# Queries and keys of the first attention group as seven products of quarters, and products added onto each other in their PSUM banks

## The chip, the core and the metric

The kernel is one launch on one core of a Trainium2 chip. A core has five engines with a queue each: TensorE (PE, matmuls; the loads of its stationary operand are shown as PEld), VectorE (DVE), ScalarE (ACT), GpSimd (POOL) and SyncE (SP), whose queue issues most of the DMAs. Each engine works its queue off in order; semaphores order the engines among each other. Matmuls write into PSUM banks of 128 x 512 float32, which DVE and ACT read; everything else lies in SBUF tiles of 128 partitions. The metric is the device time of the launch in microseconds (us), the median of several runs. A profiled execution of the same program gives the trace.

## What is computed

A decoder layer on 512 tokens of width 1024: a normed input u goes through one wide projection, whose columns are queries, keys and values of 18 attention heads in three groups of six (dilations 1, 4 and 16), a pooling branch, a state-space branch and gates; the branches are gated, added and projected, and a gated feed-forward block with a short convolution follows. What matters here is the projection of the queries, keys and values and what follows it:

```python
u = rmsnorm(x, ln1_g[i])
proj = u @ w_in[i]
q, k, v, pool_in, z, xbc, dt_raw, gate_pre = jnp.split(proj, split_idx, axis=-1)
...
scores = jnp.einsum("bhnqd,bhnkd->bhnqk", qb, kb).astype(jnp.float32) * scale + bias[:, None]
```

The result is wanted in float32 precision. Each matmul operand is therefore split into a high part (rounded to the matmul's input format) and a low part (the rest), and a product is three matmuls: high by high, high by low, low by high (`mm3`, line 229).

## The kernel before

**Jobs.** The program is a list of jobs (`program`, line 1423), most of them a block of weights with the matmuls that use it. While job n runs on PE, `prepare` (line 1641) makes the low part of job n+1's weights (`low`, L216, DVE), casts the high part of job n+2 in two halves (`cast`, L196, ACT; the halves are put after the next two steps of the job), and starts the DMA of job n+3 (`fetch`). A job may have a `form`, which is called ahead of its cast and names the tile that its weights come from, and a `then`, called behind its low part. The weight tiles rotate: two raw, three high, two low.

**Steps.** Each job calls `step` (line 157) once or more. A step advances the side work, generators in `waiting` and `running`: attention items, pooling, the state-space scan, sums. The engines' queues hold this work in the order in which the Python program records it, for PE, ACT, DVE and POOL alike. SP's queue alone is ordered by the framework.

**Seven products for eight.** A product of two matrices that are cut into quarters takes eight products of quarters, or seven of sums and differences of quarters. Here the token sides are quarters of u (256 tokens by four blocks of 128 rows) and their sums. `sums_of_u(p)` (line 403) makes them for the block pair p = 0 to 3: two reads `uf` (high plus low, L408), four half-width sums `sa` and `sb` (L326 to L329, DVE), two casts to the high parts `sah`, `sbh` (L332, L333, ACT) and two low parts `sal`, `sbl` (L335, L336, DVE). On the weight side the sums are differences of two raw quarters (`diff`, L341, DVE) of 128 x 1536 elements; the two right quarters are loaded into two tiles `w3` of a pool of two (`ypool`), the left ones are fetched as jobs' raw weights.

Two places run seven products before the change:

- `v_pair` (line 608) with `sevens` (line 344): the values of groups 1 and 2, one as left half and one as right half. A job is 2 x 12 matmuls of 384 columns, with weights moving. Its outputs are scattered by DMA (L627, SP) into the tiles `vr` in the order of the dilated groups.
- `qk_sevens(1)` (line 650): queries (left) and keys (right) of group 1. A job is 3 x 12 matmuls of 256 columns.

Each product goes to a PSUM bank of its own; ACT copies some into SBUF tiles `r1`, `r2`, `r5`, and DVE adds the others to them and adds the sums into the output tiles. Groups 0 and 2 use `qk_jobs` (line 631) instead: six chunks of 24 matmuls of 512 columns each; ACT writes the queries, scaled by 0.125, and DVE the keys.

**The order around the change.** The program runs the pooling projection (four jobs of two chunks m; the first two are unrolled in the kernel's opening), the values of group 0 (`v_jobs(0)`, two jobs of 400 columns, four banks), the queries and keys of group 0, the pooling's output, `w_b`'s branch with group 0's attention beside it, four chunks of gates, the pair of values, group 1's queries and keys, and so on. The sums of u are recorded beside `w_b`'s branch, from its fourth job on. The pooling of a chunk (`pool_evac`, line 852) is a copy `pu` on ACT, then a chain of sums and short copies `psw` on POOL (two to nine operations, longer for later chunks), and two steps later `pd` (L869, DVE), a cast `pdh` (L871, ACT) and `pdl` (L872, DVE).

PSUM has two rings of four banks: `MM` for the large products and `SM` for the small ones. SBUF tiles of the side work come from a ring of 54.

Of the kernel before, what the change touches and what calls it, by code (L numbers as in the profile page):

```python
# [83 lines left out]
def trunk(ctx: ExitStack, tc, out, x, rel_bias, ln1_g, w_in, b_gate, w_a, pool_w, pool_scale, w_b,  # L84
# [255 lines left out]
    def diff(out, a, b):  # L340
        dve.tensor_tensor(out, a, b, OP.subtract)  # L341
        return out

    def sevens(quarter, c, side, W, emit):

        r1, r2, r3, r5 = {}, {}, {}, {}

        def job(j, load, form, use):  # L350
            def body(ws):
                wh, wl = ws
                parts = side(j)
                for i in range(2):
                    ps = MM("pb")
                    o = slice(i * P, (i + 1) * P)
                    mm3(ps[:, :c], lambda k: wh[:, k, :], lambda k: wl[:, k, :],
                        lambda k: parts[k][0][:, o], lambda k: parts[k][1][:, o], range(4), flip=True)
                    use(i, ps[:, :c])
                step()  # L360
            new = Job([load] if load is not None else [], 4, c, body)
            new.form = form
            if load is None:
                new.load = lambda: None
            return new

        def keep(r, name):
            def use(i, ps):
                r[i] = T(name)[:, :c]
                act.copy(r[i], ps)  # L370
            return use

        def p5(i, ps):
            keep(r5, "r5")(i, ps)
            dve.tensor_tensor(r2[i], r2[i], ps, OP.add)

        def p6(i, ps):
            dve.tensor_tensor(r1[i], r1[i], ps, OP.add)
            emit(0, 1, i, r1[i], r2[i])

        def p7(i, ps):
            r3[i] = T("r3")[:, :c]
            dve.tensor_tensor(r3[i], r1[i], ps, OP.add)
            emit(1, 1, i, r3[i], r5[i])

        one = job("A11", quarter(0, 0), None, keep(r1, "r1"))
        two = job("A12", quarter(1, 0), None, lambda i, ps: emit(0, 0, i, r1[i], ps))
        three = job(4, None, lambda: W[1], keep(r2, "r2"))
        one.then = lambda: diff(one.raw, W[0], one.raw)
        three.then = lambda: diff(W[0], W[1], W[0])  # L390
        two.then = lambda: diff(W[1], W[1], one.raw)
        yield one
        yield three
        yield two
        yield job(1, None, lambda: one.raw, p5)
        yield job(2, None, lambda: W[1], p6)
        yield job(3, None, lambda: W[0], p7)
        yield job("A22", None, lambda: diff(two.raw, two.raw, W[1]),
                  lambda i, ps: emit(1, 0, i, r3[i], ps))

# [18 lines left out]
    QUARTER = {"A11": (0, LO), "A12": (1, LO), "A22": (1, HI)}  # L419

# [187 lines left out]
    def v_pair():  # L608

        c, W = C_V + 384, []  # L610
        rows_ = lambda c0: w_in[:, c0:c0 + 384].rearrange("(k two p) c -> two p k c", two=2, p=P)
        quarter = lambda two, h: rows_(c + 384 * h)[two]

        def load():
            for two in range(2):
                W.append(ypool.tile([P, 4, S], F32, name="w3", tag="xs")[:, :, :384])
                sp.dma_start(W[two], quarter(two, 1))

        def emit(hi, right, i, a, ps):
            g, tb = 1 + right, 2 * hi + i  # L620
            t = T(f"v{g}")
            dve.tensor_tensor(t[:, :384], a, ps, OP.add)

            for n in range(4):
                if (g, n) not in V:
                    V[g, n] = T(f"vr{g}")
                sp.dma_start(V[g, n][32 * tb:32 * tb + 32, :384], t[n:P:4, :384])  # L627

        return load, sevens(quarter, 384, side_u, W, emit)
# [20 lines left out]
    def qk_sevens(g):  # L650


        W = []
# [3 lines left out]
        r1, r2, r3, r5 = {}, {}, {}, {}  # L657

        def load():
            for two in range(2):  # L660
                W.append(ypool.tile([P, 4, S], F32, name="w3", tag="xs")[:, :, :384])
                sp.dma_start(W[two], quarter(two, 1))

        def job(j, raw, form, use):
            def body(ws):
                wh, wl = ws
                parts = side_u(j)
                for i, ms in enumerate(chunks):
                    ps = MM("pq")
                    for n, m in enumerate(ms):  # L670
                        o = slice(m * P, (m + 1) * P)
                        mm3(ps[:, 256 * n:256 * n + 256], lambda k: wh[:, k, o], lambda k: wl[:, k, o],
                            lambda k: parts[k][0], lambda k: parts[k][1], range(4))
                    use(i, ps[:, :256 * len(ms)])
                step()
            new = Job([raw] if raw is not None else [], 4, 384, body)
            new.form = form
            if raw is None:
                new.load = lambda: None
            return new  # L680

        def keep(r):
            def use(i, ps):
                r[i] = T("rq")[:, :ps.shape[-1]]
                act.copy(r[i], ps)
            return use

        def emit(which, hi, i, a, b):

            for n, m in enumerate(chunks[i]):  # L690
                if (which, g, m) not in QK:
                    QK[which, g, m] = T(f"{which}{g}")
                view = (grouped if which == "q" else plain)(QK[which, g, m], g)
                piece = lambda t: perm(t[:, 256 * n:256 * n + 256], g)
                dve.tensor_tensor(view[:, :, 64 * hi:64 * hi + 64], piece(a), piece(b), OP.add)

        def p5(i, ps):
            keep(r5)(i, ps)
            dve.tensor_tensor(r2[i], r2[i], ps, OP.add)

        def p6(i, ps):
            dve.tensor_tensor(r1[i], r1[i], ps, OP.add)
            emit("k", 0, i, r1[i], r2[i])

        def p7(i, ps):
            r3[i] = T("rq")[:, :ps.shape[-1]]
            dve.tensor_tensor(r3[i], r1[i], ps, OP.add)
            emit("k", 1, i, r3[i], r5[i])

        one = job("A11", quarter(0, 0), None, keep(r1))  # L710
        two = job("A12", quarter(1, 0), None, lambda i, ps: emit("q", 0, i, r1[i], ps))
        three = job(4, None, lambda: W[1], keep(r2))
        one.then = lambda: diff(one.raw, W[0], one.raw)
        three.then = lambda: diff(W[0], W[1], W[0])
        two.then = lambda: diff(W[1], W[1], one.raw)
        return load, [one, three, two, job(1, None, lambda: one.raw, p5), job(2, None, lambda: W[1], p6),
                      job(3, None, lambda: W[0], p7), job("A22", None, lambda: diff(two.raw, two.raw, W[1]),
                                                          lambda i, ps: emit("q", 1, i, r3[i], ps))]

    def attend(g):  # L720
# [7 lines left out]
        def item(h, nb, bank):  # L728
# [21 lines left out]
            if g == 0 and total == 384:  # L750
                dve.tensor_tensor(sb[:, :256], ps[:, :256], b, OP.add)
                dve.tensor_tensor(sb[:, 256:384], ps[:, 256:384], b[:, P:], OP.add)
# [3 lines left out]
            else:  # L756
                n = len(bank)
                dve.scalar_tensor_tensor(sb.rearrange("p (n c) -> p n c", n=n),
                                         ps.rearrange("p (n c) -> p n c", n=n), 0.125 if g == 1 else 1.0,
# [663 lines left out]
    def program():  # L1423
        yield from jobs_a(w_in, C_POOL, 8, uhk, ulk, KD, pool_evac)
        yield Call(lambda: waiting.append(rows_of_bias()))
        yield from v_jobs(0)
        yield from qk_jobs(0)
        yield from pool_out_job()
        yield Call(lambda: attend(0))
        yield Call(lambda: waiting.insert(3, ssd_prep()))  # L1430
        for i, job in enumerate(branch_jobs(1, w_b, YB, 8, more=range(7))):
# [269 lines left out]
```

## Time and profile before

| | us |
|---|---|
| Median of 3 runs (1032.75 to 1033.57) | 1032.86 |
| The profiled execution | 1032.69 |
| Its span, first to last instruction | 1030.9 |
| Mean granted PE clock | 0.999 |

The page names engines as above; L12 is line 12 of the kernel. A row of a timeline gives the start, the duration, the engine, the line, the operation, `out<-in` by the program's names, sizes, and in brackets how long the engine had waited before it and for whom. Operations of one engine overlap by some 0.1 us at their ends, so that the pitch from start to start is shorter than the duration. A row of grouped instructions gives the count, the busy time and the mean of one in nanoseconds. A row of windows gives each engine's busy time in the stretch.

### The profile page before, as it was taken

To read this page: it belongs to the slowest core of one execution; us is meant where nothing else is said; L and a number is where in the kernel's file an instruction comes from. 1 tells how busy PE (TensorE), PEld (TensorE's weight loads), DVE (VectorE), ACT (ScalarE), POOL (GpSimd) and SP (SyncE) were. 2 spreads that over 40 slices of the span, in tenths; PEclk is the share of its full clock that TensorE was granted. 3 is DMA by queue.
4 is the path that set the end of the run, shared out by engine and by line. 5 is a ranking of instruction groups with operands and counts; after the bars stand their busy time and mean duration, and the time that the engine had idled before them with its cause. 6 is when DMAs were issued, how large, how long until landed. Compare 5 with 4: busy or idle time off the path is not lost.

```text
span 1030.9 us, 13254 instructions
## 1 busy us (share of the span) xinstructions
PE 1019.8 (99%) x5276; PEld 858.0 (83%) x5276; DVE 702.7 (68%) x932; ACT 490.2 (48%) x784; POOL 132.8 (13%) x114
## 2 busy tenths in 40 slices
PE   8999999999999999999999999999999999999997
PEld 8998877899888887788888888898888888888885
DVE  6553566788756648666688856767778668685756
ACT  6432545454674363567575324545444434433434
POOL 1770000000000001100044501101111100111002
PEclk9999999999999999999999999999999999999999
DMA  8444312034322354551253625543232233421322
GB/s 270 135 129 137 108 57 75 31 88 138 123 82 82 93 158 108 133 144 44 80 151 128 203 82 203 171 142 121 82 122 83 84 117 112 138 82 41 123 82 82
DMA packets 113357, 117.62 MB, mean 114 GB/s; under 512 B 5236, under 2 KB 97207, under 8 KB 113296
## 3 DMA queue, kind: packets, MB, share of 16 engines
q1 hardware_dynamic: 112703, 115.92, 36.4%
q8 instruction: 41, 0.67, 0.3%
q10 hardware_dynamic: 592, 0.86, 0.2%
q14 instruction: 21, 0.16, 0.1%
HBM read 112.97 MB, written 2.22 MB: 112 GB/s over the span
## 4 chain that ended last, share of the span: by engine, by line
PE 91%; DVE 4%; ACT 3%; issue 1%; DMA 1%; ACTq 0%; DVEq 0%
PE pa L237 30%; PE pu L237 22%; PE pb L237 12%; PE pd L237 7%; PE pqk L237 6%; PE pa L1552 2%; PE pq L237 2%; PE pu L1356 1%; PE ps L743 1%; PE pt L772 1%; PE ppw L237 1%; PE po L784 1%; DVE xs L1133 1%; DVE wl L216 1%; PE py L1057 1%
## 5 line engine op out<-in xcount | busy, mean ns | idle before, releaser
L216 DVE TENSOR_TENSOR wl<-raw,wh 128x2048 fp32r<-128x2048 f32 (+3 forms) x95 | 220.3, 2320 | 53.3 <-ACT wh L196 43.5
L196 ACT CAST wh<-raw 128x1024 fp32r<-128x1024 f32 (+3 forms) x188 | 187.6, 1017 | 48.3 <-DVE raw L341 18.0
L1251 DVE SCALAR_TENSOR_TENSOR hc<-pu,fcol,hc 128x510 f32<-128x510 f32 x88 | 65.8, 748 | 56.0 <-ACT hc L1248 54.4
L237 PE MATMUL pa<-uh,wh 128*128 128x512 f32 x384 | 98.4, 398 | 0.0
L237 PE MATMUL pa<-ul,wh 128*128 128x512 f32 x384 | 94.9, 389 | 0.0
L237 PE MATMUL pa<-uh,wl 128*128 128x512 f32 x384 | 94.8, 389 | 0.0
L237 PEld LDWEIGHTS pa<-ul,wh 128*128 128x128 f32 x384 | 72.1, 188 | 15.1
L237 PEld LDWEIGHTS pa<-uh,wl 128*128 128x128 f32 x384 | 72.1, 188 | 15.0
L237 PE MATMUL pu<-uh,wh 128*128 128x512 f32 (+1 forms) x352 | 83.6, 379 | 0.0
L237 PE MATMUL pu<-uh,wl 128*128 128x512 f32 (+1 forms) x352 | 83.5, 379 | 0.0
L237 PE MATMUL pu<-ul,wh 128*128 128x512 f32 (+1 forms) x352 | 83.5, 379 | 0.0
L237 PEld LDWEIGHTS pa<-uh,wh 128*128 128x128 f32 x384 | 70.3, 188 | 14.8 <-issue 1.0
L237 PEld LDWEIGHTS pu<-ul,wh 128*128 128x128 f32 x352 | 64.2, 188 | 12.5
L237 PEld LDWEIGHTS pu<-uh,wl 128*128 128x128 f32 x352 | 64.2, 188 | 12.5
L237 PEld LDWEIGHTS pu<-uh,wh 128*128 128x128 f32 x352 | 64.1, 188 | 12.4
L1248 ACT ACTIVATE hc<-pu,fcol,fcol 128x512 f32<-128x512 f32 x40 | 31.2, 780 | 80.5 <-PE pu L237 80.5
L1256 POOL TENSOR_TENSOR hc<-hc 128x512 f32<-128x512 f32 x22 | 30.8, 1402 | 289.1 <-DVE hc L1251 252.0
L1025 POOL TENSOR_TENSOR xd<-xc,dtz 128x512 f32<-128x512 f32 x6 | 6.4, 1063 | 355.9 <-issue 307.5
L765 ACT ACTIVATE sb<-sb,nmls 128x128 f32<-128x128 f32 (+1 forms) x72 | 30.1, 419 | 30.4 <-DVE nmls L762 17.7
L1149 ACT ACTIVATE sg<-pa,col 128x512 f32<-128x512 f32 x24 | 16.5, 688 | 45.5 <-PE pa L237 45.4
L1253 ACT ACTIVATE hc<-hc 128x512 f32<-128x512 f32 x22 | 13.9, 632 | 39.9 <-DVE hc L1251 39.9
L907 DVE SCALAR_TENSOR_TENSOR xs<-pa,col,xs 128x509 f32<-128x509 f32 (+2 forms) x24 | 18.0, 749 | 18.7 <-ACT xs L903 18.2
(373 smaller groups left out, 1868.0 us busy)
## 6 DMA issues: line engine op xcount, KB each, us to landing
raw<-in_w_in_dram SPq DMA_DIRECT2D x25, 1024.0 KB, 5.5
raw<-in_ffn_w_up_dram SPq DMA_DIRECT2D x22, 1024.0 KB, 5.2
raw<-in_w_o_dram SPq DMA_DIRECT2D x8, 1024.0 KB, 6.6
raw<-in_ffn_w_down_dram SPq DMA_DIRECT2D x8, 1024.0 KB
raw<-in_w_in_dram SPq DMA_DIRECT2D x14, 512.0 KB, 3.9
raw<-in_w_in_dram SPq DMA_DIRECT2D x6, 768.0 KB
raw<-in_w_b_dram SPq DMA_DIRECT2D x4, 1024.0 KB, 5.2
al<-ad SPq DMA_DIRECT2D x16, 256.0 KB, 7.7
```

The lines of the kernel that those rows point to most:

```text
L196: act.copy(job.high[:, :, o], job.raw[:, :, o])
L216: (eng or dve).tensor_tensor(l[:, :, o], job.raw[:, :, o], h[:, :, o].bitcast(F32), OP.subtract)
L237: pe.matmul(ps, l, r, start=first and n == 0, stop=last and n == total - 1, skip_group_check=onto)
L743: pe.matmul(pss[i][:, o:o + w * P], q[r, n * P:(n + 1) * P], k[r, kb * P:(kb + w) * P], start=True, stop=True)
L765: act.activation(sb[:, off:off + w * P], sb[:, off:off + w * P], AF.Exp, bias=nm[:, n, h:h + 1], accum_out=ls[:, n, h:h + 1])
L907: dve.scalar_tensor_tensor(t[:, sh:], ps[:, :S - sh], col[:, o_cw + 12 * k + m:o_cw + 12 * k + m + 1], t[:, sh:], OP.mult, OP.add)
L1149: act.activation(s, ps, AF.Sigmoid, bias=col[:, o:o + 1])
L1248: act.activation(t, ps, AF.Identity, bias=ff["c1"][:, ff["b"] + m:ff["b"] + m + 1], scale=fw(2, m))
L1251: dve.scalar_tensor_tensor(t[:, sh:], ps[:, :S - sh], fw(k, m), t[:, sh:], OP.mult, OP.add)
L1253: act.activation(t, t, AF.Silu)
L1256: pool.tensor_tensor(a, a, t, OP.mult)
L1552: pe.matmul(first[2 * n + j][:, lo:hi], a[:, k, j * P:(j + 1) * P], b[:, k, lo:hi], start=a is wh and b is uh and k == 0, stop=a is wl and ...
```

## The change

`sevens` and the old body of `qk_sevens` go; both users now call one function, `in_banks`. It keeps four banks for its seven jobs: two A (the two halves of the product's output) and two B. The seven products come in another order, and those that have a part in common are added onto each other in the bank: B takes product 5, then product 3 onto it, later product 2 afresh; A takes product 1, then 6, 7 and 4 onto it. Behind each half product the bank is read: `outs` copies it into the output tile (ACT) where it is the first part of that output, and adds it there (DVE) where it is the second. The differences of weights (`diff`) are called between the first and the second half of a job, and the first of them by a call of its own, ahead of the job before.

Group 0's queries and keys now take this way too, in place of `qk_jobs(0)`. For that the sums of u are made a first time already during the pooling projection (from its fourth job on); they are made a second time at the old place. Group 0's weight quarters are loaded by two calls behind the pooling, and each later user loads its quarters by two calls. The scaling by 0.125 moves for group 0 into the operation that adds the bias to the scores.

```diff
+    def in_banks(quarter, c, outs, chunks=None):
+        W, A, B = [], [], []
+        def load():
+            two = len(W)
+            W.append(ypool.tile([P, 4, S], F32, name="w3", tag="xs")[:, :, :c])
+            sp.dma_start(W[two], quarter(two, 1))
+        def job(j, raw, form, banks, use, onto=False, between=None):
+            def body(ws):
+                wh, wl = ws
+                parts = side_u(j)
+                if not A:
+                    for b in (B, A):
+                        b.extend(MM("pq") for _ in range(2))
+                for i in range(2):
+                    for n, m in enumerate(chunks[i] if chunks else (i,)):
+                        o = slice(m * P, (m + 1) * P)
+                        if chunks:
+                            mm3(banks[i][:, 256 * n:256 * n + 256], lambda k: wh[:, k, o],
+                                lambda k: wl[:, k, o], lambda k: parts[k][0], lambda k: parts[k][1],
+                                range(4), onto=onto or n > 0)
...
+                    outs(*use, i, banks[i][:, :256 * (n + 1) if chunks else c])
+                    if i == 0 and between:
+                        between()
+                    step()
...
+        one = job("A11", quarter(0, 0), None, A, (0, 0, False), between=lambda: diff(W[0], W[1], W[0]))
+        five = job(1, None, lambda: W[0], B, (1, 1, False),
+                   between=lambda: diff(one.raw, W[0], one.raw))
+        three = job(4, None, lambda: W[1], B, (1, 0, False), onto=True)
+        six = job(2, None, lambda: W[0], A, (1, 0, True), onto=True,
+                  between=lambda: diff(W[1], two.raw, W[0]))
+        seventh = job(3, None, lambda: one.raw, A, (1, 1, True), onto=True)
+        two = job("A12", quarter(1, 0), None, B, (0, 0, True))
+        four = job("A22", None, lambda: W[1], A, (0, 1, False), onto=True)
+        return load, lambda: diff(W[0], W[0], one.raw), [one, five, three, six, seventh, two, four]
...
+                if more:
+                    dve.tensor_tensor(view, view, piece, OP.add)
+                else:
+                    act.copy(view, piece)
...
     def program():
-        yield from jobs_a(w_in, C_POOL, 8, uhk, ulk, KD, pool_evac)
+        load, first, qk = qk_sevens(0)
+        for i, job in enumerate(jobs_a(w_in, C_POOL, 8, uhk, ulk, KD, pool_evac)):
+            if i == 3:
+                yield Call(lambda: running.extend(after(p, sums_of_u(p)) for p in range(4)))
+            yield job
         yield Call(lambda: waiting.append(rows_of_bias()))
-        yield from v_jobs(0)
-        yield from qk_jobs(0)
+        yield Call(load)
+        yield Call(load)
+        for i, job in enumerate(v_jobs(0)):
+            if i == 1:
+                yield Call(first)
+            yield job
+        yield from qk
         yield from pool_out_job()
...
-        load, pair = v_pair()
-        yield Call(load)
-        yield from gate_jobs(1, 0, SPLIT)
-        loads, qk = qk_sevens(1)
+        yield Call(loadv)
+        yield Call(loadv)
+        for i, job in enumerate(gate_jobs(1, 0, SPLIT)):
+            if i == 1:
+                yield Call(firstv)
+            yield job
+        load, first, qk = qk_sevens(1)
         for i, job in enumerate(pair):
+            if i in (4, 6):
+                yield Call(load)
+            if i == 6:
+                yield Call(first)
             yield job
-            if i == 4:
-                yield Call(loads)
         yield from qk
```

More of the change, by code (lines that the diff above doesn't have):

```diff
@@ L342, in diff @@
         return out
[L344 to L399, printed above, removed]
     US = {}
@@ L608, in v_pair, with outs @@
     def v_pair():
-        c, W = C_V + 384, []
+        c = C_V + 384
         rows_ = lambda c0: w_in[:, c0:c0 + 384].rearrange("(k two p) c -> two p k c", two=2, p=P)
[L612 to L619, printed above, removed]
-            g, tb = 1 + right, 2 * hi + i
-            t = T(f"v{g}")
-            dve.tensor_tensor(t[:, :384], a, ps, OP.add)
+        kept = {}
+        def outs(right, hi, more, i, ps):
+            g, tb = 1 + right, 2 * hi + i
+            if more:
+                t = kept[g, tb]
+                dve.tensor_tensor(t[:, :384], t[:, :384], ps, OP.add)
+            else:
+                t = kept[g, tb] = T(f"v{g}")
+                act.copy(t[:, :384], ps)
+                if right or not hi:
+                    return
             for n in range(4):
@@ L627, in emit @@
                 sp.dma_start(V[g, n][32 * tb:32 * tb + 32, :384], t[n:P:4, :384])
-        return load, sevens(quarter, 384, side_u, W, emit)
+        return in_banks(lambda two, h: rows_(c + 384 * h)[two], 384, outs)
     def qk_jobs(g):
@@ L656, in qk_sevens, with outs @@
         chunks = ((0, 1), (2,))
[L657 to L688, printed above, removed]
+        def outs(right, hi, more, i, ps):
+            which = "qk"[right]
             for n, m in enumerate(chunks[i]):
@@ L692, in emit @@
                     QK[which, g, m] = T(f"{which}{g}")
[L693 to L718, printed above, removed]
+                view = (plain if right else grouped)(QK[which, g, m], g)
+                piece = ps[:, 256 * n:256 * n + 256]
+                if g == 0:
+                    view = view[:, 2 * hi:2 * hi + 2] if not right else QK[which, g, m][:, 256 * hi:256 * hi + 256]
+                    piece = piece.rearrange("p (r j) -> p r j", r=2) if not right else piece
+                else:
+                    view, piece = view[:, :, 64 * hi:64 * hi + 64], perm(piece, g)
+                if more:
+                    dve.tensor_tensor(view, view, piece, OP.add)
+                else:
+                    act.copy(view, piece)
+        return in_banks(quarter, 384, outs, chunks)
     def attend(g):
@@ L1430, in program @@
         yield Call(lambda: waiting.insert(3, ssd_prep()))
+        loadv, firstv, pair = v_pair()
         for i, job in enumerate(branch_jobs(1, w_b, YB, 8, more=range(7))):
```

15 lines of the change are left out of this document (11 added, 4 removed).

## The prediction

> **What bounds the kernel now.** I read the page's busy times first, then the list of who waited for whom on PE, then the timelines of single engines.
>
> ```profile
> span 1030.9 us, 13254 instructions
> PE 1019.8 (99%) x5276; PEld 858.0 (83%) x5276; DVE 702.7 (68%) x932; ACT 490.2 (48%) x784; POOL 132.8 (13%) x114
> ...
> PE pq L237 <- DVE wl L216: 0.3, 1, 0.3
> ```
>
> PE is busy 99% of the span, and in the stages that the change touches its whole list of waits is that one of 0.3 us. A matmul less is time gained, and any lateness of another engine that reaches PE is time lost, one for one. So there are two questions: how much PE work goes, and whether DVE, ACT and the DMA queue still deliver in time. The profiled execution took 1032.69 us, 1.79 more than its span and 0.17 less than the median.
>
> **PE's gain.**
>
> ```profile
> 77.85 1.98 PE L237 MATMUL pqk<-uh,wh 128*128 128x512 f32 x8
> ...
> 110.49 0.62 PE L237 MATMUL ppw<-pdh,wh 128*128 128x512 f32 x2
> ...
> 235.31 0.64 PE L237 MATMUL pq<-uh,wh 128*128 128x256 f32 x4
> 235.78 0.64 PE L237 MATMUL pq<-ul,wh 128*128 128x256 f32 x4
> ...
> 210.35 0.85 PE L237 MATMUL pb<-wh,sbh 128*128 128x384 f32 x4
> 211.04 0.85 PE L237 MATMUL pb<-wh,sbl 128*128 128x384 f32 x4
> ```
>
> Group 0's queries and keys are 6 x 24 matmuls of 512 columns, 77.85 to 110.49: 32.64 us. They become 7 products x 3 chunks x 12 = 252 matmuls of 256 columns. Group 1 runs that shape already: four in 0.48 us, 0.120 each, so 30.24 us. Gain 2.4 us: not 1/8, because 256 columns take 0.120 and not half of 0.227. The number of matmuls of the other groups stays. Adding onto a bank instead of starting it afresh costs PE nothing that I can price; it takes 9 of 18 DVE adds out of each query-key group. That is relief on an engine that PE hardly waits for, so I book no gain for it.
>
> **What is new on DVE ahead of group 0.** The products need the sums of u before their second job. In the built order of the changed kernel, eight reads uf, sixteen half-width sums, eight low parts and a first difference of weights are queued between the pooling's own DVE work, from 56.5 us on. Their prices, by rows of the same operations later in the kernel (the pitch from start to start counts, as DVE runs them back to back):
>
> ```profile
> 173.79 1.28 DVE L408 TENSOR_TENSOR uf<-uh,ul 128x512 f32<-128x512 f32 x2
> 175.00 0.42 DVE L751 TENSOR_TENSOR sb<-ps,b 128x256 f32<-128x256 f32 x1
> ...
> 176.05 0.42 DVE L326 TENSOR_TENSOR sa<-uf 128x256 f32<-128x256 f32 x1
> ...
> 177.51 1.29 DVE L408 TENSOR_TENSOR uf<-uh,ul 128x512 f32<-128x512 f32 x2
> ...
> 189.99 0.68 DVE L335 TENSOR_TENSOR sal<-sa,sah 128x512 fp32r<-128x512 f32 x1
> 190.59 0.68 DVE L336 TENSOR_TENSOR sbl<-sb,sbh 128x512 fp32r<-128x512 f32 x1
> ...
> 201.27 1.76 DVE L341 TENSOR_TENSOR raw<-w,raw 128x1536 f32<-128x1536 f32 x1
> 202.94 0.68 DVE L1151 TENSOR_TENSOR yo<-yo,sg 128x512 f32<-128x512 f32 x1
> ```
>
> Two reads 1.21, four half sums 1.46, one low part 0.60, one difference 1.67; a low part of weights (wl) of 1536 columns, the same width, 1.7.
>
> PE reaches job two (product 5, built name five) at 77.85 + 36 x 0.12 = 82.2, and wants the low half of the fourth sum (sal of p = 3) at its eighth matmul, 83.0. What DVE has queued before that, with what held it in the run before:
>
> ```profile
> 55.51 1.03 DVE L872 TENSOR_TENSOR pdl<-pd,pdh 128x512 fp32r<-128x512 f32 x1 [0.69 <-ACT pdh L871]
> 58.15 1.51 DVE L869 SCALAR_TENSOR_TENSOR pd<-psw,pu 128x512 f32<-128x512 f32 x1 [1.61 <-POOL psw L863]
> 60.56 0.81 DVE L872 TENSOR_TENSOR pdl<-pd,pdh 128x512 fp32r<-128x512 f32 x1 [0.90 <-ACT pdh L871]
> 61.30 1.81 DVE L216 TENSOR_TENSOR wl<-raw,wh 128x1600 fp32r<-128x1600 f32 x1
> 65.94 1.51 DVE L869 SCALAR_TENSOR_TENSOR pd<-psw,pu 128x512 f32<-128x512 f32 x1 [2.83 <-POOL psw L863]
> ...
> 69.08 1.14 DVE L548 COPY rv<-psr 6x512 f32<-6x512 f32 x2
> 72.26 0.69 DVE L869 SCALAR_TENSOR_TENSOR pd<-psw,pu 128x512 f32<-128x512 f32 x1 [2.04 <-POOL psw L863]
> 73.64 0.69 DVE L872 TENSOR_TENSOR pdl<-pd,pdh 128x512 fp32r<-128x512 f32 x1 [0.69 <-ACT pdh L871]
> ```
>
> The best case, with nothing stretched: from 56.45, reads 1.2; pd and pdl of chunk 5 at their old times, to 61.2; four sums 1.5, reads 1.2, wl 1.75, four sums 1.5, reads 1.2: 68.3. Pd of chunk 6, ACT's cast and pdl 2.0; the copies rv 1.1; two low parts 1.2; four sums 1.5; reads 1.2: 75.3. Chunk 7 2.0, the difference 1.7, wl of the first product 1.7, two low parts 1.2, four sums 1.5, two low parts 1.2, wl of five 1.7, the next difference 1.7, the low part 0.7: 88.6. That is 5.6 us after PE wants it, so even then the change nets 5.6 - 2.4 = 3.2 us slower.
>
> **POOL makes it later.** POOL still runs the pooling chains of chunks 5 to 7, and the rows say that it and DVE don't read two tiles at once:
>
> ```profile
> 49.68 0.69 DVE L872 TENSOR_TENSOR pdl<-pd,pdh 128x512 fp32r<-128x512 f32 x1 [1.24 <-ACT pdh L871]
> 50.29 2.66 DVE L216 TENSOR_TENSOR wl<-raw,wh 128x1600 fp32r<-128x1600 f32 x1
> ...
> 49.81 1.45 POOL L860 TENSOR_TENSOR psw<-psw 128x508 f32<-128x508 f32 x1
> 51.21 1.78 POOL L861 COPY psw<-psw 128x4 f32<-128x4 f32 x1
> ...
> 61.50 2.50 POOL L860 TENSOR_TENSOR psw<-psw 128x508 f32<-128x508 f32 x1
> ...
> 65.86 1.04 POOL L860 TENSOR_TENSOR psw<-pu 128x511 f32<-128x511 f32 x1
> ...
> 72.01 0.22 POOL L863 TENSOR_TENSOR psw<-psw,ramp 128x16 f32<-128x16 f32 x1
> ```
>
> The same wl takes 2.66 us at 50.29, beside POOL's sum that ends at 51.26, and 1.81 at 61.30, where POOL's sum is the one that stretches, to 2.50. A copy of four elements takes 1.78 while wl runs. They hand over operation by operation: POOL got in between two DVE operations at 50.3. So I add both lists up. From 56.5, POOL has about 1.4 of chunk 5, and two chains of about 5.5 each (65.86 to 72.23 less two copies held 0.46): 12.4. DVE up to pd of chunk 6: six reads 3.6, chunk 5 1.3, eight sums 2.9, wl 1.75, pd 0.6: 10.2. In turn, with some 0.1 saved at each of twenty handovers, both end at 77.0, not at 68.9 and 72.2. DVE then has, undisturbed, the rest of the list above (ACT's cast and pdl 1.3, then 1.1, 1.2, 1.5, 1.2, 2.0, 1.7, 1.7, 1.2, 1.5, 1.2, 1.7, 1.7, 0.7): 19.7, though psw of chunk 7 is there by then. The low part is there at 96.5, **13.5 us late**. I take this value, since the new operations have two tiles as inputs like those stretched; the best case stays as the lower bound.
>
> Other waits on the way lie inside that one: ACT casts five's weights after the first difference (about 87), and before it, in its queue, stand chunk 7's cast and the copies that free the first product's bank (85); the first product's wl comes at 88.6. After five, DVE has 1.7 to 4 us of work a job against PE's 4.3, so nothing more is late in group 0.
>
> The Trainium skill (TensorE: Matmul & The Clock Gate, Part 1) says that about 3.4 us without work halves PE's clock until 3.4 us of work have passed; every row here has the clock at 1.00, so no run shows it. By it the first product would run slow after its idle 6 us, but ends about 94, before the low part comes.
>
> **The pair of value groups and group 1.** The built queue of SP issues group 1's second weight quarter behind 24 scattering DMAs of values; before, both quarters stood behind 8.
>
> ```profile
> 219.06 5.76 SPq L627 DMA_DIRECT2D vr<-v  x8
> 226.79 2.04 SPq L662 DMA_DIRECT2D w<-in_w_in_dram  x2
> ...
> 236.75 10.75 SPq L627 DMA_DIRECT2D vr<-v  x16
> ...
> DMA to landing us min/median/max: 5.2/5.2/5.2
> ...
> L196 ACT CAST wh<-w 128x768 fp32r<-128x768 f32 x11 | 8.7, 833 | 4.6 <-DMA w<-in_w_in_dram 4.1 <-DVE w L341 0.6
> ```
>
> A value job is 24 matmuls, 4.16 us (0.69 for four, above). Counted from the pair's start, the fourth product's first half is added at about 15.9, since wl of the fifth stands ahead of that add on DVE. The scatters go out from 16.0 at 0.67 each; 24 of them and one quarter end at 32.5, and the second quarter lands 5.2 later, 37.7. The third product of group 1 starts at 7 x 4.16 + 2 x 4.32 = 37.8 and needs that quarter cast: two casts of 0.83 with copies of the second product's banks between and behind them in ACT's queue, 40.4. **2.6 us late**; at 0.60 a scatter and a landing of 5 it is 1, at 0.73 it is 4. The attention's scaling moves into an operation of about the same length; PE doesn't wait for it.
>
> Sum: 1030.9 - 2.4 + 13.5 + 2.6 = 1044.6 of span, 1046.4 with what lies around it, 1046.6 beside the median. I say 1046.
>
> **Rivals.**
> - POOL doesn't stretch the new operations: stall 5.6 instead of 13.5, 1038.7. For it: at 61.30 DVE kept its pace while POOL paid. Against: 50.29, and pd with 1.51 for 0.69 at 58.15 and 65.94. Chance 0.15.
> - Group 1's quarter arrives in time: 1044.0. It is inside the forecast's own range.
> - The clock rule above bites on five as well: its last 29 matmuls at half pace, 29 x 0.12 = 3.5 more, 1050. Chance 0.08.
> - Faster: one mechanism, that DVE has the fourth sum by 83.0. Then only the 2.4 us remain, 1030.5. For it: DVE is busy 11.0 of 19.4 us in the stage, and waits for POOL in three gaps of 1.6 to 2.8. Against: about 30 us of listed work for 26.5 us, even unstretched. It needs the sums to cost 5.6 us less than their rows. Chance 0.06.
>
> ```profile
> 58.40:77.80 19.40, 19.40 (x105) 18.09 (x105) 10.99 (x10) 7.43 (x14) 13.19 (x18) 1.00 0.47 123
> 77.80:110.50 32.70, 32.70 (x147) 27.08 (x146) 8.08 (x5) 8.95 (x12) 0.00 (x0) 1.00 0.45 137
> ```
>
> **How the numbers follow.** Forecast (both stalls, 1042 to 1049) 0.62; the rivals as above; 0.05 for gain and stall cancelling within 0.2%; 0.04 for a further wait that I missed. The range of 8 in 10 takes in the rival without POOL's share at its upper half and the slow clock: 1038 to 1050. About 0.2% (2 us) is what a measurement can tell from no change. Faster 0.06, same 0.05, slower 0.89.
>
> **What would show it.** Right: PE idle before group 0's first product and again inside its second, waiting for DVE's wl and sal, about 13 us together; POOL's last chain ending at 77, not 72; PE waiting for ACT's cast of a quarter in group 1's third product. Wrong: PE busy straight through 77 to 100, or the stall there near 5, with reads of 0.6 beside a running POOL. A fourth sum that is done by 83 would overturn the sign.

## The result, and the profile after

The changed kernel takes 1044.97 us (median of 4 runs, 1044.52 to 1046.16) beside 1033.21 for the kernel before in the same comparison: a ratio of 1.0116, with a 95% interval of 1.0104 to 1.0128. It is slower by 11.8 us. The forecast was 1046.

First the page's span of the changed kernel, and its list of who waited for whom on PE (times: total, count, longest):

```profile
span 1042.7 us, 13531 instructions
...
PE pq L237 <- ACT dtr L596: 5.2, 1, 5.2
PE pq L237 <- DVE wl L216: 2.0, 2, 1.5
PE pq L237 <- ACT k L667: 1.8, 1, 1.8
PE pq L237 <- DVE sal L335: 1.3, 1, 1.3
```

Before, one wait of 0.3 us stood in the stages of the change. Now there are four kinds, all ahead of `pq`, the products that add in their banks. The same trace by windows, for group 0, the value pair and group 1 (the length, then the busy time of PE, PEld, DVE, ACT and POOL, then the granted clock):

```profile
77.80:120.01 42.21, 34.10 (x254) 33.37 (x253) 34.12 (x41) 20.00 (x39) 0.00 (x0) 0.88 0.40 127
215.68:244.83 29.15, 29.15 (x170) 29.15 (x169) 22.18 (x20) 13.88 (x22) 0.00 (x0) 1.00 0.27 83
244.83:278.12 33.29, 30.98 (x254) 30.37 (x253) 22.39 (x20) 15.39 (x27) 0.00 (x0) 1.00 0.44 135
```

The pair and group 1 in the kernel before:

```profile
206.16:235.31 29.15, 29.15 (x170) 29.14 (x168) 24.38 (x25) 13.22 (x20) 0.00 (x0) 1.00 0.37 106
235.31:266.12 30.81, 30.54 (x253) 30.33 (x253) 27.44 (x29) 13.90 (x20) 0.00 (x0) 1.00 0.37 112
```

Group 0 takes 42.2 us where it took 32.6, the pair 29.15 as before, group 1 33.29 where it took 30.81. So 9.5 and 2.5 us came in, at two places, and nothing in between: 12.0 beside 11.8 more of span. In the first window DVE is as busy as PE, 34.1 us, and the clock is 0.88.

PE at the start of group 0:

```profile
77.15 0.89 PE L237 MATMUL pb<-wl,uh 128*128 128x400 f32 x4
83.28 1.22 PE L237 MATMUL pq<-uh,wh 128*128 128x256 f32 x4 [5.25 <-ACT dtr L596]
...
86.90 1.22 PE L237 MATMUL pq<-uh,wl 128*128 128x256 f32 x4 [1.54 <-DVE wl L216]
87.92 1.05 PE L237 MATMUL pq<-uh,wh 128*128 128x256 f32 x4
88.77 1.05 PE L237 MATMUL pq<-ul,wh 128*128 128x256 f32 x4
...
92.99 0.52 PE L237 MATMUL pq<-sal,wh 128*128 128x256 f32 x3
94.83 0.39 PE L237 MATMUL pq<-sal,wh 128*128 128x256 f32 x1 [1.32 <-DVE sal L335]
95.06 0.64 PE L237 MATMUL pq<-sah,wl 128*128 128x256 f32 x4
```

PE goes idle for 5.25 us, then for 1.54, then for 1.32. In between, four matmuls of 256 columns take 0.85 us from start to start (87.92 to 88.77); the usual pace, 0.48, is back at 92. The granted clock of a window over those four, 87.92 to 88.77, is 0.50. What these matmuls waited for, on ACT, DVE and POOL:

```profile
82.16 0.62 ACT L822 CAST pdh<-pd 128x512 fp32r<-128x512 f32 x1 [4.56 <-DVE pd L820]
...
83.06 0.18 ACT L596 COPY dtr<-pb 128x16 f32<-128x16 f32 x1
```

```profile
66.61 2.65 DVE L216 TENSOR_TENSOR wl<-raw,wh 128x1600 fp32r<-128x1600 f32 x1
...
69.64 1.14 DVE L327 TENSOR_TENSOR sa<-sa,uf 128x256 f32<-128x256 f32 x1
...
72.21 2.36 DVE L351 TENSOR_TENSOR uf<-uh,ul 128x512 f32<-128x512 f32 x2
...
81.39 0.68 DVE L820 SCALAR_TENSOR_TENSOR pd<-psw,pu 128x512 f32<-128x512 f32 x1
...
94.10 0.68 DVE L335 TENSOR_TENSOR sal<-sa,sah 128x512 fp32r<-128x512 f32 x1
```

```profile
74.70 0.55 POOL L814 TENSOR_TENSOR psw<-psw,ramp 128x16 f32<-128x16 f32 x1
```

The wait that is named dtr is a wait for DVE. ACT's copies out of the value banks stand in its queue behind the cast `pdh` of chunk 7, and that stood 4.56 us for `pd`, which DVE did at 81.39, behind the sums. POOL had the chain of chunk 7 done at 75.25. The last low part of the sums starts on DVE at 94.10, with no bracket: DVE has no pause between 83 and 95.

SP's queue around group 1, and what DVE and PE waited for there:

```profile
232.00 5.74 SPq L622 DMA_DIRECT2D vr<-v  x8
237.79 0.58 SPq L374 DMA_DIRECT2D w<-in_w_in_dram  x1
238.47 10.02 SPq L622 DMA_DIRECT2D vr<-v  x16
248.58 0.53 SPq L374 DMA_DIRECT2D w<-in_w_in_dram  x1
```

```profile
253.72 1.76 DVE L341 TENSOR_TENSOR w<-w,w 128x1536 f32<-128x1536 f32 x1 [5.24 <-DMA w<-in_w_in_dram]
```

```profile
256.14 0.74 PE L237 MATMUL pq<-sbh,wh 128*128 128x256 f32 x4 [1.83 <-ACT k L667]
```

The second quarter goes out at 248.58, behind 24 scatters, 32.9 us after the pair's start, and lands 5.1 later. PE stands 1.83 us ahead of the third product.

### The profile page after: what moved, and what is told of

Same layout as the page of the kernel before. It is cut to its first block, busy times and chain, and to the rows that moved or that the text cites. A ratio compares the mean times of both kernels' runs of the same rounds, so it can differ in the third digit from the quotient of the medians.

```text
span 1042.7 us, 13531 instructions
## 1 busy us (share of the span) xinstructions
PE 1022.5 (98%) x5384; PEld 865.0 (83%) x5384; DVE 726.5 (70%) x961; ACT 503.4 (48%) x817; POOL 135.8 (13%) x114
## 4 chain that ended last, share of the span: by engine, by line
PE 84%; DVE 7%; ACT 3%; POOL 2%; DMA 2%; issue 1%; SPq 1%; ACTq 0%; DVEq 0%; POOLq 0%
PE pa L237 27%; PE pu L237 22%; PE pb L237 7%; PE pd L237 7%; PE pq L237 6%; PE pqk L237 3%; PE pa L1518 2%; DVE wl L216 1%; PE pu L1307 1%; POOL psw L811 1%; PE ps L694 1%; PE ppw L237 1%; PE pt L723 1%; PE po L735 1%; DMA w<-in_w_in_dram 1%
## 5 line engine op out<-in xcount | busy, mean ns | idle before, releaser
L216 DVE TENSOR_TENSOR wl<-raw,wh 128x2048 fp32r<-128x2048 f32 (+3 forms) x93 | 216.1, 2325 | 60.1 <-ACT wh L196 51.4
L196 ACT CAST wh<-raw 128x1024 fp32r<-128x1024 f32 (+3 forms) x184 | 183.5, 1015 | 38.4 <-DVE raw L341 10.9
L237 PE MATMUL pa<-uh,wh 128*128 128x512 f32 x384 | 98.4, 398 | 0.0
L1207 POOL TENSOR_TENSOR hc<-hc 128x512 f32<-128x512 f32 x22 | 30.8, 1402 | 289.1 <-DVE hc L1202 251.9
L196 ACT CAST wh<-w 128x768 fp32r<-128x768 f32 (+1 forms) x36 | 32.1, 908 | 18.0 <-DVE w L341 13.6
L216 DVE TENSOR_TENSOR wl<-w,wh 128x1536 fp32r<-128x1536 f32 (+1 forms) x18 | 35.9, 1992 | 1.7 <-ACT wh L196 1.6
```

Source lines behind the costliest of these rows:

```text
L196: act.copy(job.high[:, :, o], job.raw[:, :, o])
L216: (eng or dve).tensor_tensor(l[:, :, o], job.raw[:, :, o], h[:, :, o].bitcast(F32), OP.subtract)
L237: pe.matmul(ps, l, r, start=first and n == 0, stop=last and n == total - 1, skip_group_check=onto)
L1207: pool.tensor_tensor(a, a, t, OP.mult)
```

## The experiments

The times below are medians. The opening of the kernel also varies between profiled executions: PE waits 0.7 to 2.4 us for `diag` there, and the values of group 0 begin at 58.46 to 59.28 us. Stages are therefore compared by their own length: "stage 0" runs from the first matmul of group 0's values to the first of `w_b`'s branch (62.9 us before, 72.4 after), "group 1" from its first product to the gates behind it (30.8 and 33.3).

### Each half of the change alone

First group 0 alone, in the kernel before: the new products under a name of their own, with their early sums and quarters; `v_pair` and `qk_sevens(1)` stay as they were.

```diff
-        yield from jobs_a(w_in, C_POOL, 8, uhk, ulk, KD, pool_evac)
+        load, first, qk = qk_banks(0)
+        for i, job in enumerate(jobs_a(w_in, C_POOL, 8, uhk, ulk, KD, pool_evac)):
+            if i == 3:
+                yield Call(lambda: running.extend(after(p, sums_of_u(p)) for p in range(4)))
+            yield job
...
-        yield from qk_jobs(0)
+        yield from qk
```

> The kernel before with group 0's queries and keys alone by the new products, early sums of u included; value pair and group 1 as before. Theory (the sums come too late): the whole stage costs what the trace of the changed kernel shows there, 120.01 - 110.49 = 9.5 us, so 1033 + 9.5 = 1042.5, PE waiting for the copy dtr (about 5), the weights' low part wl (about 1.5-2) and the low part sal (about 1.3), and no wait for an ACT copy of k in group 1. Rival (the late start of the stage also delays something behind it, or the value pair is what costs): under 1040 or over 1045.

Measured: 1042.74, ratio 1.0092 (1.0075 to 1.0108). Stage 0 takes 72.4 us, 9.5 more than before, with waits of 5.2 for dtr, 2.2 for wl and 2.2 for sal; group 1 has no wait for a copy of k.

Then the rest alone: in the changed kernel, group 0's early sums, quarters and products are taken out again.

```diff
-            if i == 3:
-                yield Call(lambda: running.extend(after(p, sums_of_u(p)) for p in range(4)))
...
-        yield from qk
+        yield from qk_jobs(0)
```

> The changed kernel with group 0's queries and keys put back (6 x 24 products of 512 columns, no early sums, no early quarters); value pair and group 1 still add in their banks. Theory (the second weight quarter stands behind 24 scatters): +2.5, so 1035.5, with PE waits of about 0.4 for wl and 1.8 for the ACT copy of k in group 1 and next to none elsewhere. Rival (the nine DVE adds saved in each group are worth something, or that wait was only a follow-up of group 0's lateness): 1033 or less.

Measured: 1036.64, ratio 1.0038 (1.0023 to 1.0053). Stage 0 is back at 62.9; pair and group 1 take 62.9 together for 60.0 before, with one wait of 2.38 for the copy of k and one of 0.33 for wl. The two halves add up: 9.5 and 2.9 by the stages, beside 12.0 in the changed kernel. The medians say 9.7 and 3.6, 13.4 together beside 11.8; with intervals of some 3 us each, that is no contradiction. The second wait is no follow-up of the first.

### Without POOL's chains

```diff
-        while sh < w:
-            nxt = T("psw")
-            pool.tensor_tensor(nxt[:, sh:], cur[:, sh:], cur[:, :S - sh], OP.add)
-            pool.tensor_copy(nxt[:, :sh], cur[:, :sh])
-            cur, sh = nxt, sh * 2
-        pool.tensor_tensor(cur[:, :w], cur[:, :w], ramp[:, g, :w], OP.mult)
```

> The changed kernel with the pooling chains on POOL left out: the pooling's running sums are not formed, POOL does nothing before 80 us. Theory (DVE's list is too long even alone, and POOL lengthens it): without POOL the fourth sum's low part is ready at about 88 instead of 94.8, wl and uf run at 1.75 and 1.21; PE's waits in group 0 fall from about 8 us together plus 4 of slow clock to about 4; 1045 - 7 = 1038. Rival 1 (POOL stretches nothing that matters): 1045. Rival 2 (only POOL is to blame): all of the stall goes, 1033.

Measured: 1042.03, ratio 1.0087 (1.0072 to 1.0103). DVE and PE of this run:

```profile
66.85 0.43 DVE L327 TENSOR_TENSOR sa<-sa,uf 128x256 f32<-128x256 f32 x1
...
88.69 0.68 DVE L335 TENSOR_TENSOR sal<-sa,sah 128x512 fp32r<-128x512 f32 x1
```

```profile
89.43 0.39 PE L237 MATMUL pq<-sal,wh 128*128 128x256 f32 x1 [3.50 <-DVE sal L335]
...
90.12 1.01 PE L237 MATMUL pq<-sah,wh 128*128 128x256 f32 x4
...
93.50 0.68 PE L237 MATMUL pq<-sal,wh 128*128 128x256 f32 x4
```

With no sum on POOL the half-width sum takes 0.43 instead of 1.14, and the last low part starts at 88.69 instead of 94.10. In this execution stage 0 began 0.8 us later (59.28 for 58.50); counted from there, PE resumes behind the low part after 30.15 us instead of 36.33: POOL made DVE's list 6.2 us later. Stage 0 takes 67.7, 4.7 less than in the changed kernel and 4.8 more than before. So each rival falls: POOL mattered, and without it the list is still too long. The gain of 7 was too high by 2.3: about 1.5 is the clock, since after the wait of 3.50 four rows run at 0.85 instead of 0.48, and nothing hides them; the rest is that 6.2 were gained on DVE and not 7. The run as a whole gained only 3; in this execution group 1 lost 2 us more than in that of the changed kernel (35.4 for 33.3), by a longer wait for wl (1.19 for 0.44) and by four slow rows behind its wait for the copy of k:

```profile
252.85 0.74 PE L237 MATMUL pq<-sbh,wh 128*128 128x256 f32 x4 [1.68 <-ACT k L667]
...
255.12 1.05 PE L237 MATMUL pq<-sbh,wh 128*128 128x256 f32 x4
```

Here the pooling's running sums were left out.

### A clock kept up

```diff
+        def keep_warm():
+            ps = SM("warm")
+            for i in range(20):
+                pe.matmul(ps[:, :P], ones.bitcast(F32), ones.bitcast(F32), start=True, stop=True)
...
+        yield Call(keep_warm)
         yield from qk
```

> The changed kernel with 20 matmuls of ones by ones, of 128 columns, put on PE between the values of group 0 and its first product, into a bank that nothing reads, so that PE is not idle for the 5 us before that product. Theory (the fourth sum sets the end, at 94.8, whatever PE does before): the first product now runs at 0.48 per four matmuls, PE then waits some 5 us instead of 1.3 for sal, and what follows that wait runs slow in the open: 1045 to 1047, no gain. Rival (the slow matmuls after the 5 us of idleness are what costs): 8 products of 12 at 0.213 for 0.120 were 3 to 4 us of it, so 1041 to 1042.

Measured: 1047.33, ratio 1.0144 (1.0124 to 1.0164), 2.4 above the changed kernel and just above the range of the theory. PE:

```profile
78.05 4.63 PE L1377 MATMUL warm<-ones 128*128 128x128 f32 x40
...
95.00 0.58 PE L237 MATMUL pq<-sal,wh 128*128 128x256 f32 x1 [2.01 <-DVE sal L335]
95.38 1.06 PE L237 MATMUL pq<-sah,wl 128*128 128x256 f32 x4
```

The idle 5 us are filled, but the last low part arrives when it did, and PE resumes at 95.00 instead of 94.83. The first product starts at full pace but still meets a slow stretch behind its wait of 2.39 us for wl (granted clock 0.50 from 88.12 to 91.50), which the sums cover. A second slow stretch follows the wait for sal, 0.50 from 95.00 to 98.30, where nothing covers it: stage 0 takes 73.9, 1.5 more. In this execution group 1 lost 1.5 more as well (34.8 for 33.3), with a wait of 2.78 for the copy of k and slow rows behind it. The slow matmuls of the changed kernel lay in the shadow of the sums.

### The second quarter earlier

```diff
+        pair[6].then = load
         for i, job in enumerate(pair):
-            if i in (4, 6):
+            if i == 4:
                 yield Call(load)
```

> The changed kernel with one edit: the load of group 1's second weight quarter is issued as soon as the last reader of its buffer is queued, which puts it behind 16 scattering DMAs instead of 24 on SP's queue. Theory: it goes out some 5 us earlier, PE's wait of 1.8 for the ACT copy of k in group 1 goes and at most the 0.4 for wl stays: 1045 - 2 = 1043. Rival (that wait has another cause, such as DVE's own list or ACT's order): 1045, with the wait still there.

Measured: 1042.71, ratio 1.0093 (1.0076 to 1.0110), 2.3 below the changed kernel. SP's queue:

```profile
238.44 5.01 SPq L622 DMA_DIRECT2D vr<-v  x8
243.55 0.53 SPq L374 DMA_DIRECT2D w<-in_w_in_dram  x1
```

`then` runs behind the low part of the seventh job, the last reader of the buffer. The load goes out 5.0 us earlier, the wait for the copy of k is gone, group 1 takes 31.05 instead of 33.29.

### Both terms taken away

The two edits together: group 0 by `qk_jobs(0)`, and the early quarter.

> Group 0's queries and keys as before, value pair and group 1 by the new products, and group 1's second quarter issued early: both lost terms of the sum taken away at once. Theory: nothing is left to wait for, and the number of matmuls is that of before: 1033, same within 0.2%. If the DVE adds saved by adding in the banks were worth something, under 1031; if a third cost hides in the change, over 1035.

Measured: 1033.74 (11 runs) beside 1033.57 (15 runs), ratio 1.0006 (0.9997 to 1.0015). The list of waits on PE behind the opening:

```profile
PE pa L237 <- DVE al L797: 0.6, 1, 0.6
PE pq L237 <- DVE wl L216: 0.4, 1, 0.4
PE pcb L971 <- DVE ea L1017: 0.3, 1, 0.3
```

The same three as before, and the same time. The two stalls are the whole loss; the pair and group 1 take 59.98 us together, 59.96 before. The adds that the banks save on DVE are worth nothing that can be measured.

### Giving the sums more time

Three tries to keep group 0's products. First the pooling's output is put ahead of them, and the first difference of weights behind the values:

```diff
-        for i, job in enumerate(v_jobs(0)):
-            if i == 1:
-                yield Call(first)
-            yield job
+        yield from v_jobs(0)
+        yield Call(first)
+        yield from pool_out_job()
         yield from qk
-        yield from pool_out_job()
```

> The changed kernel with the pooling's output products (8 x 6 products, 9.5 to 11 us of PE) put between group 0's values and its queries and keys, nothing else moved. Theory: the sums have some 10 us more, so the waits for wl and sal (1.5 + 1.3) and the slow clock's part go; but the 5 us wait for the copy dtr stays, since ACT makes that copy behind the cast of chunk 7, which DVE brings late at 82; stall about 5 of 12 left, 1045 - 6.5 = 1038.5. Rival (the lateness is DVE's total work and only moves): 1044 to 1046. Rival 2 (all of it hidden): 1033.

Measured: 1043.72, ratio 1.0106 (1.0091 to 1.0121). The products themselves now run with no wait, 99.85 to 130.08: 30.2 us. But the wait for dtr stays, now in front of `ppw`, the pooling's output, and slow matmuls follow it:

```profile
83.91 1.17 PE L237 MATMUL ppw<-pdh,wh 128*128 128x512 f32 x2 [5.24 <-ACT dtr L596]
...
88.26 1.05 PE L237 MATMUL ppw<-pdl,wh 128*128 128x512 f32 x2
89.11 1.05 PE L237 MATMUL ppw<-pdh,wl 128*128 128x512 f32 x2
...
94.26 0.72 PE L237 MATMUL ppw<-pdh,wh 128*128 128x512 f32 x2 [0.96 <-DVE ybl L838]
```

```profile
91.79 1.75 DVE L216 TENSOR_TENSOR wl<-raw,wh 128x1536 fp32r<-128x1536 f32 x1
93.46 2.72 DVE L838 SCALAR_TENSOR_TENSOR ybl<-ppw,col,ybh 128x512 fp32r<-128x512 f32 x4
```

Two matmuls of 512 columns take 0.85 from start to start instead of 0.46, up to 90.82. This slow stretch is covered again: the fifth chunk of `ppw` waits until 94.26 for a bank that `ybl` frees, and DVE starts `ybl` at 93.46, right behind a low part and with no pause since 83.44. By these rows a faster PE would only have waited longer there. So DVE's list still sets the end, only at another reader. Stage 0 takes 70.95, 1.5 less than in the changed kernel, and the time lies just below the range of the first rival, that the lateness only moves. Second, the sums also start later, behind the last pooling product (with the pooling's output still ahead, and with the early quarter):

```diff
-            if i == 3:
-                yield Call(lambda: running.extend(after(p, sums_of_u(p)) for p in range(4)))
             yield job
+        yield Call(lambda: running.extend(after(p, sums_of_u(p)) for p in range(4)))
```

> Three edits beside the change: the pooling's output products come before group 0's queries and keys (as in the run above), the sums of u start after the last pooling product instead of at the fourth weight block, and group 1's second quarter is issued early. Theory: chunk 7's difference is no longer queued behind the sums on DVE, so ACT casts it in time and frees the banks, PE does not go idle at 78 and does not slow down; the sums have until about 94 and their list of some 28 us from 66 just fits; no wait in group 1: 1033 - 2.4 + 0 to 3 = 1030.5 to 1034. Rival (DVE is short of time over the whole stretch 56 to 95 and the stall only moves): 1038 to 1042.

Measured: 1043.42, ratio 1.0100 (1.0085 to 1.0115). The wait for dtr is gone, as expected. A new one takes its place, and one of 1.68 for sal follows it:

```profile
90.94 1.22 PE L237 MATMUL ppw<-pdh,wh 128*128 128x512 f32 x2 [5.69 <-DVE ybl L838]
```

```profile
88.47 1.75 DVE L216 TENSOR_TENSOR wl<-raw,wh 128x1536 fp32r<-128x1536 f32 x1
90.14 2.72 DVE L838 SCALAR_TENSOR_TENSOR ybl<-ppw,col,ybh 128x512 fp32r<-128x512 f32 x4
```

The pooling's output frees its banks by `ybl` on DVE, and `ybl` now stands behind the sums, a difference and a low part. By its sum the list fitted, but what was read soon stood behind what was read late: the stall only moved, as the rival has it, and the time is above even the rival's range of 1038 to 1042. Stage 0 takes 72.8, 0.4 more than in the changed kernel, so that beside the run with the early quarter alone (1042.71) nothing is gained. Third, with the same order and the early quarter, the sums begin early and are spread over every second step (`after(2 * p, ...)`):

> As the run before it, but the sums start at the fourth weight block as in the changed kernel and are spread, one pair of rows every second step instead of every step. Theory: two of the four sums share their time with POOL and cost some 3 us more, but DVE has 9 us more for the whole; chunk 7's difference comes 1 to 3 us late: 1031 to 1035. Rival (any sums before 72 us delay the pooling's differences as in the changed kernel): the dtr wait of 5 stays and so do 1038 to 1042.

Measured: 1041.30, ratio 1.0080 (1.0062 to 1.0098). PE at the late sum:

```profile
102.99 0.39 PE L237 MATMUL pq<-sal,wh 128*128 128x256 f32 x1 [2.69 <-DVE sal L335]
103.21 0.64 PE L237 MATMUL pq<-sah,wl 128*128 128x256 f32 x4
```

Three waits share the loss, this one, 3.05 for ybl and 1.26 for wl; the wait for dtr shrank to 0.25. The time lies in the rival's range, but not by the rival's reason, since the wait for dtr of 5 us did not stay. Stage 0 takes 69.4, 6.4 more than before, in the fastest of the four executions (1039.44): the best of the three tries, and still a loss. DVE has no room in this stretch for 15.5 us of sums (4 x (1.21 + 1.46 + 1.20), by the prediction's prices) beside the differences and low parts of the weights.

### Group 2 instead

The sums exist once anyway, beside `w_b`. So group 2 can use them with no new sums, if its products come right behind group 1's. This edit stands on the run with both terms taken away:

```diff
         yield Call(lambda: attend(1))
+        yield from qk2
+        yield Call(lambda: attend(2))
...
         yield Call(ssd_start)
-        yield from qk_jobs(2)
-        yield Call(lambda: attend(2))
```

> As the run above, and group 2's queries and keys, 6 x 24 products of 512 columns before, are also made by the seven products, right after group 1's, with the sums of u that the value pair already needs; attention of group 2 is queued there too, ahead of the gates. Theory (the change's saving on PE is real, 2.4 a group, and was lost only because the sums had to be made too early): no new sums on DVE, so 1033 - 2.4 = 1030.6 if nothing waits. Rival (the stage after it, robbed of 33 us of PE work beside which the scan of the state and attention ran, begins to wait): 1033 or more.

Measured: 1048.97, ratio 1.0153 (1.0137 to 1.0169). The time is in the rival's range:

```profile
PE pa L237 <- ACT yth L1086: 5.9, 3, 2.6
PE pbt L943 <- ACT xcv L1027: 3.1, 1, 3.1
```

The old products of group 2 were the PE work beside which the state's scan began; now PE waits for its start (xcv) and for its end (yth), and 2.2 us for attention's `sb`. Two repairs followed: half of the gates moved behind the start of the scan,

> As the run with group 2, and the second half of the gates of branch 1 (22 us of PE) comes after the start of the state's scan instead of ahead of the blocks of x, B and C, so that the scan's start again has PE work beside it. Theory: the wait of 3 at the scan's start goes; the scan still has 11 us less PE work beside it than before and its end may still be late by some us: 1033 to 1040. If the 33 us of cover were all that was missing, 1031 to 1033; rival (attention of group 2 queued early is what disturbs): 1046 or more.

and the items of the scan were started step by step as well:

> As the run above, with the eight scan items started one step after the other instead of every second step (the free steps between them held group 2's attention, which is now done earlier). Theory: the scan's end comes before its reader and the waits for the last rows yth go: 1030.6 to 1033. Rival (DVE, with more of the scan at once, is late for the gates): no better than the run above.

Measured: 1037.57, ratio 1.0040 (1.0025 to 1.0054), and 1047.57, ratio 1.0137 (1.0122 to 1.0152). The first repair took the waits for xcv and yth away and left others of 2.5 and 1.7 us inside the scan and the 2.2 for `sb`; its time lies in the expected range of 1033 to 1040. The second made it worse: PE then waits 5.4 and 3.7 us for `xc` of DVE, so packing the scan only brings DVE's lateness forward. No version was found that beats the kernel before.

## Why the prediction was right

**PE's gain, 2.4 us.** Right: the run with no wait inside the products has them in 30.23 us against 30.24 worked out, and 32.64 before.

**The sums are late for product five.** Right in the mechanism. Forecast: the last low part at 96.5, 13.5 us late. Measured: PE resumes at 94.83, 11.8 late, and stage 0 loses 11.9 - 2.4 = 9.5 where 11.1 was forecast. The lower bound of the working, the list with nothing stretched, had the low part done at 88.6. The run without POOL's chains has it done at 89.37 (88.69 and 0.68), in an execution whose stage 0 began 0.8 us later than the one that the working is built on: the same within 0.1. The idle time that the working named as a sign, about 13 us together, was 8.1 (5.25, 1.54 and 1.32); most of the rest of the 11.8 went into the first product at its slow pace.

**POOL's part was mis-sized.** The forecast added both lists up and let them end together at 77.0; POOL's last chain ended at 75.25, so the handing over cost 1.75 us less up to there, and 6.2 in all instead of 7.9 (96.5 - 88.6). The list behind it was priced well: 19.7 forecast, 19.6 measured (75.17, the end of chunk 6's pd, to 94.78). A small slip is in the sum: 77.0 and 19.7 make 96.7. Stretched are the half sums (1.14 for 0.43), the reads (2.36 for 1.29) and the wl (2.65), but not every operation: `sa` from two reads kept 0.41 at 69.19. The rival in which POOL stretches nothing falls by these rows; its price, 5.6 - 2.4 = 3.2, is what stage 0 of the run without POOL shows (4.8) less its 1.5 of slow clock.

**Where PE stood.** The forecast saw two more waits in the shadow, the banks freed by ACT at 85 and the first wl at 88.6; they came at 83.28 and 86.90. The profile books most of the idle time on them (5.25 and 1.54) and only 1.32 on sal. Yet sal sets the end: filling the first wait with other matmuls left the end where it was.

**The clock.** After 5.25 us without work four matmuls take 0.85 instead of 0.48, at a granted clock of 0.50. The Trainium skill (TensorE: Matmul & The Clock Gate, Part 1) says that an idle window halves the clock, and the trace agrees. As forecast, this was hidden in the changed kernel, and the rival in which it bites on five as well falls there. It does bite in the runs without POOL's chains and with the filled wait, by 1.5 us each in stage 0, where the rival had 3.5.

**The second quarter.** Forecast 2.6 (issue at 32.5 after the pair's start, landing at 37.7), measured 2.5 (32.9 and 38.0). Issuing it 5 us earlier gives 2.2 back.

**The sum.** Span 1044.6 forecast, 1042.7 measured; the difference is POOL's part. The rival of a faster kernel needed the fourth sum by 83.0 and missed it by 11.8 us, even without POOL by 5.6 (PE resumes at 89.43 there, in a stage that began 0.8 later). The adds saved on DVE were booked at nothing, and that is what the run with both terms taken away shows.

## What to carry to other kernels

Work taken from an engine that is busy all the time is only worth what the helpers' deadlines leave of it: add up what the new operands cost on the helping engine between the moment when it can start and the moment when they are read, and compare it with that engine's idle time in just this stretch, not over the kernel. In queues that are worked off in order, ask also what stands behind the new work: here the pooling's difference, then ACT's copies, then the banks, and in the repairs `ybl`. And a wait that the profile books on one name may lie in the shadow of another one; fill it or remove it before believing that it is worth its length. The same goes for slow matmuls: what they cost shows only where no later wait covers them.

## What the runs showed of the hardware

The slow clock does not follow the length of a wait alone. Waits of 2.38, 2.69 and 3.05 us (group 1 of the run with group 0 as before; twice with the spread sums) were followed by matmuls at full pace, at a granted clock of 1.00. One of 2.01 (the filled wait) was followed by four rows at 0.85, and so was one of 1.68 (group 1 of the run without POOL's chains), at 0.50 and 0.51. The slow stretches behind single waits of 1.68 to 3.50 us lasted some 3.4 us: 254.1 to 257.5 and 90.1 to 93.5 without POOL's chains, 95.0 to 98.4 with the filled wait. The one behind the 5.69 us for `ybl` lasted 6.1 (90.94 to 97.08). The Trainium skill (TensorE: Matmul & The Clock Gate, Part 1) has the activity looked at in a free-running window, and an idle one of about 3.4 us as what slows the clock. The waits of 1.68 and 2.01 us are shorter than that, and here the measurement decides. A free-running window that need not be empty throughout would fit these numbers; this was argued from them and not tried by itself.
